# Memory outputs as high and low parts, and where the late gates end, in a hybrid decoder layer

## The chip, the cores and the metric

The kernel runs on one core of one Trainium2 chip. The metric is the device time of one execution in microseconds (us). A matrix product runs on TensorE (PE), with its weight loads beside it (PEld); VectorE is DVE, ScalarE ACT, GpSimd POOL, and SyncE (SP) issues most of the DMAs. Each of these engines works off its own queue of instructions in order.

## The reference

One decoder layer for 1024 tokens of width 1024. From one input projection come a sparse attention (8 heads of 64), a convolution branch and a cross-attention into 256 memory tokens (4 heads of 128). Each branch is projected to the width, weighted by a sigmoid gate, and the three are added; then follow the output projection and a SwiGLU feed-forward part.

```python
xn = rms_norm(x, norm_mix)
proj = xn @ w_in            # q, k, v, gates, conv inputs, memory queries, 3 merge gates
br_nsa = nsa_attention(q, kc, vc, ks, vs, kw, vw, gate) @ w_nsa_out
br_conv = silu(layer_norm(conv(glu(conv_in)))) @ w_conv_out
p_m = softmax(einsum('bshd,bmhd->bhsm', qm, km) * MEM_HEAD_DIM ** -0.5)
br_mem = einsum('bhsm,bmhd->bshd', p_m, vm).reshape(b, s, MEM_WIDTH) @ w_mem_out
gm = sigmoid(g_merge).reshape(b, s, N_BRANCH, D_MODEL)
h = x + (gm[:, :, 0] * br_nsa + gm[:, :, 1] * br_conv + gm[:, :, 2] * br_mem) @ w_out
return h + (silu(hn @ w_gate) * (hn @ w_up)) @ w_down      # hn = rms_norm(h, norm_ffn)
```

## The kernel before

**Arithmetic.** All is float32. A large product is made of three products of parts: an operand is split into a high part (a cast on ACT, L131) and a low part (the difference, L132, on DVE or POOL); `mm3` multiplies high by high, high by low and low by high (L146). An operand that was stored to DRAM whole has to be split again when it is loaded.

**Buffers.** `slab` is a pool of 16 buffers of 1 MB (128 partitions x 2048 words), used for the parts of activations; `wslab` (3) and `fslab` (2) hold split weights; `stage` (2 buffers named st) takes whole inputs of `unit` before they are split; `t4` and `t2` are small working tiles. PSUM banks come from `bank` (seven of them in turn), from `fbank` (one, the tile pf) or from `anybank` (all eight). A transfer into a buffer waits until the last reader of the former content is done.

**Order.** A scheduler orders the instructions of each engine by priorities and a model of their times; `follow(a, b)` and `add_manual_dep` add an order between two instructions. So an edit at one place can move others.

**Stages.** Input projections and key/value work; the memory attention in eight units of 256 tokens and two heads; the sparse attention in 16 groups (`for n in range(2 * NT)`: 128 tokens and one of two key groups each); the merge of the three branches (`branches`: memory, sparse attention, convolution); output projection; feed-forward part.

- A unit of the memory attention loads its queries from DRAM (L588) and splits them (`mem_qT`), makes scores, maxima and exponentials (`mem_softmax`, L609), turns the weights over through DRAM (`mem_squares`, `mem_load`), and multiplies by the values (`mem_out`). A copy on DVE (L645) takes the output from PSUM, and it is stored whole to `md`.
- The 24 merge gates (three branches of 8 column blocks, each `xn` by 128 columns of `w_in` in two halves of 24 products) are filler: they have a low priority. The first 12 (`N_EARLY`) may come anywhere, the late 12 are held to products of the attention (`anchors`): the j-th product of the late gates comes behind the anchor at which the share of the attention's work times 100/SPREAD is reached, with SPREAD = 97. A gate's half is copied from PSUM on ACT (L979, tile fz) and stored to `zd`.
- In attention, weights are transposed on PE against an identity (L918 for blocks, L904 for the compressed branch), taken from PSUM as parts (L131, L132), and multiplied by values. Some weights go through DRAM instead: `square_store` (L844) and `square_load` (L856, tensor `wd`). A group's output goes to `od` (L892).
- The memory merge loads the outputs `md` whole into st (L271), splits them into four slabs, and multiplies by `w_mem_out` (four units of 256 columns); each column block also loads its gate from `zd` (L1048) and takes its sigmoid (L1049). The casts of the last two outputs are held behind the last of `cmps`, the casts of the compressed branch's weights. The inputs of the next merge (from `od`) take the same path through st. The convolution's layer norm loads its inputs `ud` (L987).

## Time and profile before

| what | value |
|---|---|
| runs, us | 1701.01, 1700.6, 1700.25 (median 1700.6) |
| the profiled execution, us | 1696.93, of which the span is 1695.2 |
| mean granted clock of PE | 0.991 |
| PE busy | 97% of the span |
| chain that ended last | PE 53%, DVE 3%, DMA 2%, POOL 2%, ACT 1% |
| data moved | 262.11 MB, mean 155 GB/s |

In a row of the profile, `ps<-slab,fsl 128*128 128x512 x28` is output, operands, tile and shape, and the number of instructions; what stands in brackets is the idle time of the engine just before, and what ended it. In rows by stage come for each engine the busy time and (x) the number of instructions, then the clock granted to PE as a share of the full one, and the share and rate of the DMA. A group's mean time of a product can be above its step in a row of many, since products overlap: the step is the time of the row divided by its count.

### The profile page before, as it was taken

What the parts mean: (1) busy time and instruction counts of PE and PEld (TensorE: products, weight loads), DVE (VectorE), ACT (ScalarE), POOL (GpSimd) and SP (SyncE); (2) the same over time, 40 slices, a digit from 0 to 9 for tenths busy, and PEclk for the clock granted to TensorE, in tenths of its full rate; (3) what the DMA queues carried; (4) which work ended last, traced back from release to release, by engine and by line L of the source; (5) the groups of instructions that cost most, each with busy time, mean ns of one, the idle gap of its engine ahead of it and who ended that gap; (6) DMA issues with size and microseconds to landing.
All of it is one profiled execution on the core that took longest, in us unless ns stands there. A gap on an engine that the chain in (4) does not pass through costs nothing.

```text
span 1695.2 us, 22465 instructions
## 1 busy us (share of the span) xinstructions
PE 1650.6 (97%) x7904; PEld 1373.2 (81%) x7904; DVE 1064.8 (63%) x1800; ACT 729.8 (43%) x1343; POOL 642.6 (38%) x551
## 2 busy tenths in 40 slices
PE   7999999899999999998989999999999999999999
PEld 6887898787888888876867888888888888888887
DVE  6279888679556666865368626765545454466665
ACT  6311444342467767765356424532222323233332
POOL 0010012352267768764015401366556776400000
PEclk9999999999999999998989999999999999999999
DMA  8134345564255655545464313333233545793763
GB/s 282 40 96 132 124 143 174 160 194 136 77 160 147 166 171 166 165 133 178 170 215 150 107 50 132 96 114 118 91 109 118 168 143 178 268 402 125 228 234 123
DMA packets 247254, 262.11 MB, mean 155 GB/s; under 512 B 23956, under 2 KB 171716, under 8 KB 246118
## 3 DMA queue, kind: packets, MB, share of 16 engines
q1 hardware_dynamic: 240230, 248.10, 46.3%
q10 hardware_dynamic: 6912, 12.59, 2.0%
q8 instruction: 62, 1.02, 0.2%
q14 instruction: 50, 0.41, 0.1%
HBM read 181.99 MB, written 78.64 MB: 154 GB/s over the span
## 4 chain that ended last, share of the span: by engine, by line
PE 53%; DVE 3%; DMA 2%; POOL 2%; ACT 1%; issue 1%; SPq 0%; ACTq 0%; DVEq 0%; POOLq 0%
PE ps L146 34%; PE ps L1382 11%; PE pf L146 6%; PE pf L1382 1%; PE ps L918 1%; DMA st<-in_w_nsa_out_dram 1%; POOL slab L132 0%; DVE slab L132 0%; PE ps L236 0%; DMA t<-zd 0%; DMA st<-in_w_mem_out_dram 0%; DMA wd<-wsl 0%; POOL slab L729 0%; DVE t L1062 0%; POOL slab L1063 0%
## 5 line engine op out<-in xcount | busy, mean ns | idle before, releaser
L146 PE MATMUL ps<-slab,wsl 128*128 128x512 f32 (+1 forms) x1628 | 361.7, 381 | 0.0
L146 PEld LDWEIGHTS ps<-slab,wsl 128*128 128x128 f32 x1628 | 295.7, 188 | 59.7 <-issue 1.0
L146 PE MATMUL pf<-slab,fsl 128*128 128x512 f32 x1152 | 293.1, 395 | 2.0 <-ACT fz L979 1.8
L146 PEld LDWEIGHTS pf<-slab,fsl 128*128 128x128 f32 x1152 | 211.0, 188 | 43.9 <-ACT fz L979 3.4
L146 PE MATMUL ps<-slab,fsl 128*128 128x512 f32 x768 | 184.7, 395 | 10.5 <-ACT fsl L131 7.7
L146 PEld LDWEIGHTS ps<-slab,fsl 128*128 128x128 f32 x768 | 145.5, 190 | 43.5 <-ACT fsl L131 8.4
L447 DVE SCALAR_TENSOR_TENSOR slab<-slab,cw 128x1019 f32<-128x1019 f32 (+16 forms) x120 | 163.5, 1367 | 1.8
L146 PE MATMUL ps<-slab,slab 128*128 128x512 f32 (+1 forms) x616 | 150.7, 380 | 6.2 <-ACT slab L131 3.5
L1278 DVE TENSOR_TENSOR t<-ps,t 128x512 f32<-128x512 f32 x127 | 86.9, 688 | 108.1 <-PE ps L146 106.8
L146 PE MATMUL ps<-wsl,slab 128*128 128x512 f32 (+1 forms) x690 | 149.1, 365 | 0.5 <-DVE slab L228 0.3
L146 PEld LDWEIGHTS ps<-slab,slab 128*128 128x128 f32 x616 | 111.2, 190 | 29.4 <-ACT slab L131 4.0
L146 PEld LDWEIGHTS ps<-wsl,slab 128*128 128x128 f32 x690 | 117.4, 190 | 20.7 <-DVE t L645 0.6
L1382 PE MATMUL ps<-wsl 128*128 128x512 f32 x495 | 118.6, 389 | 0.0
L1382 PEld LDWEIGHTS ps<-wsl 128*128 128x128 f32 x495 | 92.9, 188 | 19.3
L132 DVE TENSOR_TENSOR wsl<-st,wsl 128x1024 fp32r<-128x1024 f32 x57 | 77.6, 1361 | 44.3 <-ACT wsl L131 43.4
L131 ACT CAST wsl<-st 128x1024 fp32r<-128x1024 f32 x58 | 60.9, 1051 | 89.4 <-PE ps L146 36.2
L146 PE MATMUL ps<-slab,qt 128*128 128x384 f32 (+6 forms) x400 | 93.8, 338 | 2.8 <-DVE sm L799 2.5
L146 PE MATMUL ps<-t,slab 128*128 128x256 f32 (+1 forms) x404 | 92.8, 332 | 2.4 <-DVE t L132 1.6
L1063 POOL TENSOR_TENSOR slab<-slab,t 128x512 f32<-128x512 f32 x32 | 48.1, 1521 | 113.4 <-DVE t L1062 113.4
L131 ACT CAST wsl<-t 128x1024 fp32r<-128x1024 f32 x43 | 45.3, 1054 | 90.6 <-POOL t L128 36.4
L1291 POOL TENSOR_TENSOR t<-t,t 128x512 f32<-128x512 f32 x21 | 40.0, 1906 | 112.4 <-DVE t L1278 44.9
L132 DVE TENSOR_TENSOR t<-ps,t 128x512 fp32r<-128x512 f32 (+2 forms) x96 | 60.9, 639 | 30.6 <-ACT t L131 29.7
(252 smaller groups left out, 2810.5 us busy)
## 6 DMA issues: line engine op xcount, KB each, us to landing
t<-in_w_down_dram SPq DMA_DIRECT2D x70, 256.0 KB, 4.1
fst<-in_w_in_dram SPq DMA_DIRECT2D x24, 512.0 KB, 4.5
zd<-fz ACTq DMA_DIRECT2D x48, 256.0 KB, 3.4
slab<-wd SPq DMA_DIRECT2D x24, 512.0 KB, 4.4
t<-zd SPq DMA_DIRECT2D x24, 512.0 KB, 3.4
st<-in_w_gate_dram SPq DMA_DIRECT2D x22, 512.0 KB, 3.9
st<-in_w_up_dram SPq DMA_DIRECT2D x22, 512.0 KB, 4.2
ad<-t SPq DMA_DIRECT2D x44, 256.0 KB, 2.8
```

The lines of the kernel that those rows point to most:

```text
L131: m = nc.scalar.copy(hi, src)
L132: return m, (eng or nc.vector).tensor_tensor(lo, src, hi.bitcast(F32), op=OP.subtract)
L146: m = nc.tensor.matmul(o, a, b, start=start, stop=stop)
L447: return nc.vector.scalar_tensor_tensor(acc[:, s:], u[:, :S - s], cw[:, ct, 30 - s:31 - s], acc[:, s:], op0=OP.mult, op1=OP.add)
L918: nc.tensor.transpose(b[:, j - j0, h, :], tiles[h][:, j * P:(j + 1) * P], ident)
L1063: nc.gpsimd.tensor_tensor(a, a, z, op=OP.add)
L1278: nc.vector.tensor_tensor(o, a_, b_, op=OP.add)
L1291: nc.gpsimd.tensor_tensor(u4, u4, c22, op=OP.mult)
L1382: nc.tensor.matmul(B[t], a_, b_, start=start and k == 0 and j == 0, stop=k == FH - 1 and j == 2, skip_group_check=True)
```

## The change

Memory outputs are now split where they are made: `mem_out` casts the output from PSUM into the slab that held the weights, makes the low part on DVE, and stores both to `md`, which is twice as large (16 stores of 256 KB for 8). They are loaded as parts, 1 MB each, straight into four slabs (`mem_in`, L955) in the last step of attention that makes scores, behind the last square load written by then; the casts and low parts of the memory merge's inputs and `cmps` are gone. SPREAD is 84 instead of 97, and all gates use `fbank`. Queries of the memory attention are loaded two units ahead (`mem_qload`), and their casts come behind the exponentials of the unit before. The `ud` loads follow the last square load, the sigmoids the last exponential, and the second halves of the memory merge's first four blocks may use any bank. The number of products is the same.

```diff
--- before
+++ after
@@ -33,3 +33,3 @@
 N_EARLY = 12
-WB, SPREAD = 6, 97
+WB, SPREAD = 6, 84
 TAP_LEAD = 12
@@ -198,3 +198,3 @@
     od = drp.tile([4, P, S], F32, tag="od", name="od")
-    md = drp.tile([4, P, S], F32, tag="md", name="md")
+    md = drp.tile([4, P, 2, S], F32, tag="md", name="md")
     qraw = drp.tile([2, NT, P, 512], F32, tag="qraw", name="qraw")
@@ -265,3 +265,3 @@
 
-    def unit(src, shape, alloc=wslab, eng=None, load=False, after=None):
+    def unit(src, shape, alloc=wslab, eng=None, load=False):
         if alloc is fslab:
@@ -272,5 +272,3 @@
         w = alloc([2] + shape)
-        m, _ = split(w[:, 0], w[:, 1], st, eng)
-        if after is not None:
-            follow(m, after, "cast behind")
+        split(w[:, 0], w[:, 1], st, eng)
         return (w, ld.ins) if load else w
@@ -584,9 +582,15 @@
 
-    def mem_qT(hp, tp):
-        QM, raw = t4([2, 2, 2, 4, 32], F32R), t2([2, 4, 2, 32])
+    def mem_qload(u):
+        raw = t2([2, 4, 2, 32])
         for tt in range(2):
-            nc.sync.dma_start(raw[:, tt],
-                              qt_m[2 * tp + tt, :, :, :, 64 * hp:64 * hp + 64].rearrange("c r a (h s) -> (c r) a h s", h=2))
+            nc.sync.dma_start(raw[:, tt], qt_m[2 * (u % 4) + tt, :, :, :, 64 * (u // 4):64 * (u // 4) + 64].rearrange(
+                "c r a (h s) -> (c r) a h s", h=2))
+        return raw
+
+    def mem_queries(raw):
+        QM = t4([2, 2, 2, 4, 32], F32R)
         for tt in range(2):
-            split(QM[:, 0, tt], QM[:, 1, tt], raw[:, tt].rearrange("p a h s -> p h a s"), nc.gpsimd)
+            m, _ = split(QM[:, 0, tt], QM[:, 1, tt], raw[:, tt].rearrange("p a h s -> p h a s"), nc.gpsimd)
+            if exps:
+                follow(m, exps[-1], "queries behind the exponentials")
         return QM
@@ -643,5 +647,7 @@
                     VM[:, 1, mb, hh * P:(hh + 1) * P], ph, pl, mb == 0, mb == 1)
-        om = t2([2, 256])
-        nc.vector.tensor_copy(om, o)
-        nc.sync.dma_start(md[2 * hp:2 * hp + 2, :, tp * 256:(tp + 1) * 256].rearrange("h p t -> p h t"), om)
+        om = [PT[:, hl, 0].rearrange("p a h t s -> p (a h t s)").rearrange("p (h t) -> p h t", h=2) for hl in range(2)]
+        split(om[0], om[1], o)
+        for hl in range(2):
+            nc.sync.dma_start(md[2 * hp:2 * hp + 2, :, hl, tp * 256:(tp + 1) * 256].rearrange("h p t -> p h t"),
+                              om[hl].bitcast(F32))
 
@@ -649,7 +655,11 @@
 
-        QM, PT = {0: mem_qT(0, 0)}, {}
+        raws, PT = [mem_qload(0), mem_qload(1)], {}
+        QM = mem_queries(raws.pop(0))
         for u in range(8):
+            if u < 6:
+                raws.append(mem_qload(u + 2))
+            pm = mem_softmax(u // 4, u % 4, QM)
             if u < 7:
-                QM[u + 1] = mem_qT((u + 1) // 4, (u + 1) % 4)
-            mem_squares(u // 4, u % 4, mem_softmax(u // 4, u % 4, QM[u]))
+                QM = mem_queries(raws.pop(0))
+            mem_squares(u // 4, u % 4, pm)
             queries(ws, u, 1, rqn)
@@ -731,2 +741,3 @@
     QS, OB, QN, PC, WT, WP, WF, anchors, behind, tails = {}, {}, {}, {}, {}, {}, {}, [], [], []
+    squares = []
     wd = drp.tile([2 * NT, 20, 32, 4, P], F32, tag="wd", name="wd")
@@ -855,4 +866,5 @@
         n = o.shape[1]
-        nc.sync.dma_start(o.bitcast(F32).rearrange("p j a h q -> p j (a h q)"),
-                          wd[2 * i + g, 4 * j0:4 * (j0 + n)].rearrange("(j b) k a q -> (b k) j (a q)", b=4))
+        squares.append(nc.sync.dma_start(
+            o.bitcast(F32).rearrange("p j a h q -> p j (a h q)"),
+            wd[2 * i + g, 4 * j0:4 * (j0 + n)].rearrange("(j b) k a q -> (b k) j (a q)", b=4)).ins)
 
@@ -905,3 +917,3 @@
             pt = t2([4, P], F32R)
-            cmps.append(split(pt[:64], pt[64:], b[:64])[0].ins)
+            split(pt[:64], pt[64:], b[:64])
             m = mm(o.rearrange("p h q -> p (h q)"), vcmp[:, g, :], pt.rearrange("p h q -> p (h q)"), True, False)
@@ -926,3 +938,2 @@
 
-    cmps = []
     load_q(0, 0)
@@ -940,2 +951,6 @@
                 turn_q((n + 1) // 2, (n + 1) % 2)
+            if step == 4 * (2 * NT - 1) + 3:
+                mem_in = [slab([2, S]) for k in range(4)]
+                for k in range(4):
+                    follow(nc.sync.dma_start(mem_in[k].bitcast(F32), md[k]), squares[-1], "behind the squares")
             tiles = scores(i, g, br, hp)
@@ -971,3 +986,3 @@
             for h_ in range(2):
-                ps = (bank if n_ > 20 and h_ else fbank)([512])
+                ps = fbank([512])
                 for k in range(KT):
@@ -986,3 +1001,3 @@
         for ct in range(4):
-            nc.sync.dma_start(U[ct][:, 1], ud[ct])
+            follow(nc.sync.dma_start(U[ct][:, 1], ud[ct]), squares[-1], "behind the last squares")
 
@@ -1032,3 +1047,3 @@
     branches = ((2, w_mem_out), (0, w_nsa_out), (1, w_conv_out))
-    nxt, conv = [unit(md[k], [S], alloc=slab, after=cmps[-1] if k > 1 else None) for k in range(4)], []
+    nxt, conv = mem_in, []
     steps = layer_norm(conv)
@@ -1048,6 +1063,6 @@
                 nc.sync.dma_start(zz, zd[br, d_])
-                nc.scalar.activation(zz, zz, AF.Sigmoid)
+                follow(nc.scalar.activation(zz, zz, AF.Sigmoid), exps[-1], "behind the last exponential")
                 for half in range(2):
                     z = zz[:, half * 512:(half + 1) * 512]
-                    ps = (anybank if n_ else bank)([512])
+                    ps = (anybank if n_ or dp < 2 and half else bank)([512])
                     for k in range(4):
```

**ACT in the memory attention**, at the fourth unit. L609 (L613 after) is an exponential, L341 and L345 (L339, L343) belong to another projection, and `t4<-t2 128x256` on L131 is the cast of half a unit's queries. Before:

```order
L341 COPY t2_312_2203<-ps_311_2178 128x512
L345 ACTIVATE t2_313_2204<-ps_311_2178 128x512
L131 CAST t4_301_2132<-t2_302_2133 128x256
L609 ACTIVATE t4_303_2140,sm_306_2143<-ps_308_2145,sm_305_2142 128x256 x2
L609 ACTIVATE t4_303_2140,sm_306_2143<-ps_309_2153,sm_305_2142 128x256 x2
```

After:

```order
L131 CAST slab_285_2036<-ps_299_2117 128x512
L613 ACT_TABLE_LOAD
L613 ACTIVATE t4_302_2139,sm_305_2142<-ps_307_2144,sm_304_2141 128x256 x2
L613 ACTIVATE t4_302_2139,sm_305_2142<-ps_308_2152,sm_304_2141 128x256 x2
L131 CAST t4_309_2170<-t2_286_2038 128x256 x2
```

The query cast stood ahead of the exponentials and stands behind them now; before them comes the cast of a memory output from PSUM (`slab_285<-ps_299`), which is new.

**PE where the last group's blocks are transposed** (L918 before, L930 after). Rows with t4 and a slab are products by values. Before:

```order
L918 MATMUL ps_1261_6442<-identr_107,slab_1225_6266 128x128 x4
L904 MATMUL ps_1259_6433<-identr_107,t2_1224_6265 64x128 x2
L146 MATMUL ps_1213_6207<-t4_1255_6410,slab_393_2677 128x512
L918 MATMUL ps_1263_6454<-identr_107,slab_1225_6266 128x128 x4
L918 MATMUL ps_1265_6466<-identr_107,slab_1225_6266 128x128 x4
L146 MATMUL ps_1213_6207<-slab_1212_6204,slab_393_2677 128x512
L146 MATMUL ps_1213_6207<-t4_1255_6410,slab_393_2677 128x512
L146 MATMUL ps_1213_6207<-slab_1212_6204,slab_393_2677 128x512
L146 MATMUL ps_1213_6207<-t4_1235_6305,slab_393_2677 128x512 x2
L918 MATMUL ps_1267_6478<-identr_107,slab_1225_6266 128x128 x4
L146 MATMUL ps_1258_6432<-t2_1260_6438,vcmp_136 128x512
```

After, where the slabs 1237 to 1240 are memory outputs, fsl_1438 a unit of memory weights:

```order
L930 MATMUL ps_1257_6458<-identr_107,slab_1217_6274 128x128 x4
L916 MATMUL ps_1255_6449<-identr_107,t2_1216_6273 64x128 x2
L146 MATMUL ps_1205_6215<-t4_1251_6426,slab_386_2684 128x512
L930 MATMUL ps_1259_6470<-identr_107,slab_1217_6274 128x128 x4
L930 MATMUL ps_1261_6482<-identr_107,slab_1217_6274 128x128 x4
L146 MATMUL ps_1440_8132<-slab_1237_6366,fsl_1438_8125 128x512 x2
L146 MATMUL ps_1441_8146<-slab_1237_6366,fsl_1438_8125 128x512 x2
L146 MATMUL ps_1443_8163<-slab_1237_6366,fsl_1438_8125 128x512 x2
L146 MATMUL ps_1205_6215<-slab_1204_6212,slab_386_2684 128x512
L146 MATMUL ps_1205_6215<-t4_1251_6426,slab_386_2684 128x512
```

The first transpositions were followed by products of the group before alone; now six products of the memory merge stand behind the third. The last gate products were further on in the queue:

```order
L146 MATMUL pf_1421_7970<-slab_23_196,fsl_1420_7967 128x512
L146 MATMUL pf_1421_7970<-slab_24_197,fsl_1420_7967 128x512 x6
L146 MATMUL pf_1421_7970<-slab_25_198,fsl_1420_7967 128x512 x6
L146 MATMUL pf_1421_7970<-slab_26_199,fsl_1420_7967 128x512 x6
L146 MATMUL ps_1423_7998<-slab_64_405,fsl_1420_7967 128x512
L146 MATMUL ps_1423_7998<-slab_65_406,fsl_1420_7967 128x512 x6
L146 MATMUL ps_1477_8296<-slab_1430_8032,fsl_1475_8290 128x512 x2
L146 MATMUL ps_1478_8310<-slab_1430_8032,fsl_1475_8290 128x512 x2
L146 MATMUL ps_1481_8331<-slab_1430_8032,fsl_1475_8290 128x512 x2
L146 MATMUL ps_1482_8345<-slab_1430_8032,fsl_1475_8290 128x512 x2
L146 MATMUL ps_1477_8296<-slab_1430_8032,fsl_1475_8290 128x512
```

These are rows in the memory merge before: pf_1421 and ps_1423 are gates (by fsl_1420), ps_1469 to ps_1482 the merge; fsl_1475 is the fourth unit of memory weights. After, this is the place:

```order
L146 MATMUL ps_1461_8270<-slab_1238_6367,wsl_1446_8193 128x512 x3
L146 MATMUL ps_1461_8270<-slab_1239_6368,wsl_1446_8193 128x512 x3
L146 MATMUL ps_1461_8270<-slab_1240_6369,wsl_1446_8193 128x512 x3
L146 MATMUL ps_1465_8292<-slab_1237_6366,fsl_1463_8286 128x512 x2
L146 MATMUL ps_1466_8306<-slab_1237_6366,fsl_1463_8286 128x512 x2
L146 MATMUL ps_1469_8327<-slab_1237_6366,fsl_1463_8286 128x512 x2
L146 MATMUL ps_1470_8341<-slab_1237_6366,fsl_1463_8286 128x512 x2
```

No gate stands there. The last gate products are now these, ahead of the last group's values:

```order
L146 MATMUL pf_1419_8014<-slab_62_403,fsl_1416_7983 128x512 x6
L146 MATMUL pf_1419_8014<-slab_63_404,fsl_1416_7983 128x512 x6
L146 MATMUL pf_1419_8014<-slab_64_405,fsl_1416_7983 128x512
L146 MATMUL ps_1142_5945<-t4_1165_6042,slab_386_2684 128x512
L146 MATMUL pf_1419_8014<-slab_64_405,fsl_1416_7983 128x512 x5
L930 MATMUL ps_1212_6249<-identr_107,slab_1155_6003 128x128 x4
L146 MATMUL pf_1419_8014<-slab_65_406,fsl_1416_7983 128x512 x6
L146 MATMUL ps_1224_6296<-slab_383_2680,qt_1153_5999 128x448 x2
```

So the gates end some 120 rows earlier against the fourth unit of weights, here fsl_1463.

**SP around the loads of the memory outputs.** L271 loads into st, L844 (L855) and L856 (L867) are square stores and loads, L892 (L904) stores a group's output. Before:

```order
L271 DMA st_1431_8035<-md_141 128x1024
L844 DMA wd_3285<-wsl_1211_6200 32x16x128 x4
L844 DMA wd_3285<-wsl_1194_6137 32x4x128 x4
L856 DMA slab_1257_6429<-wd_3285 128x2x512 x2
L271 DMA st_1433_8040<-md_141 128x1024
L271 DMA st_1435_8045<-md_141 128x1024
L892 DMA od_140<-t2_1256_6425 64x4x128
L271 DMA st_1437_8050<-in_w_mem_out_dram 128x4x256
L856 DMA t4_1269_6490<-wd_3285 128x512
L271 DMA st_1449_8127<-in_w_mem_out_dram 128x4x256
L271 DMA st_1457_8195<-in_w_mem_out_dram 128x4x256
```

After:

```order
L904 DMA od_140<-t2_1194_6180 64x4x128
L867 DMA t4_1227_6313<-wd_3293 128x512
L955 DMA slab_1237_6366<-md_141 128x2048
L955 DMA slab_1238_6367<-md_141 128x2048
L955 DMA slab_1239_6368<-md_141 128x2048
L955 DMA slab_1240_6369<-md_141 128x2048
L271 DMA st_1437_8123<-in_w_mem_out_dram 128x4x256
L271 DMA st_1445_8191<-in_w_mem_out_dram 128x4x256
L855 DMA wd_3293<-wsl_1203_6208 32x16x128 x4
L855 DMA wd_3293<-wsl_1186_6145 32x4x128 x4
L867 DMA slab_1253_6445<-wd_3293 128x2x512 x2
L904 DMA od_140<-t2_1252_6441 64x4x128
```

The four loads of `md` were spread over the last two groups, 512 KB each; now they stand in a row, 1 MB each, ahead of the last two square stores and the last large square load, with two loads of weights (st) behind them.

## The prediction

> **What bounds the kernel now.** I read the page first, then the busy time by stage, then what TensorE (PE) waits for, then the timeline at each wait.
>
> ```profile
> span 1695.2 us, 22465 instructions
> PE 1650.6 (97%) x7904; PEld 1373.2 (81%) x7904; DVE 1064.8 (63%) x1800; ACT 729.8 (43%) x1343; POOL 642.6 (38%) x551
> core 0: us, PE busy (x) PEld busy (x) DVE busy (x) ACT busy (x) POOL busy (x), PEclk, DMA share, GB/s
> 300.00:450.00 150.00, 142.76 (x692) 118.01 (x691) 110.45 (x174) 53.23 (x129) 51.72 (x44) 0.99 0.47 143
> 450.00:750.00 300.00, 294.15 (x1622) 250.33 (x1621) 198.55 (x711) 214.35 (x540) 218.41 (x236) 1.00 0.55 158
> 750.00:800.00 50.00, 41.86 (x206) 33.40 (x206) 31.34 (x69) 28.81 (x51) 24.34 (x19) 0.86 0.48 150
> 800.00:846.00 46.00, 46.00 (x205) 37.74 (x204) 13.13 (x17) 14.10 (x16) 2.77 (x2) 1.00 0.52 186
> 846.00:875.00 29.00, 21.44 (x82) 16.79 (x82) 17.77 (x21) 15.71 (x17) 0.00 (x0) 0.82 0.69 218
> 875.00:925.00 50.00, 47.19 (x202) 37.54 (x201) 42.99 (x37) 30.07 (x29) 23.11 (x14) 1.00 0.49 159
> 925.00:1695.00 770.00, 766.50 (x3413) 634.99 (x3412) 427.40 (x509) 258.74 (x340) 289.26 (x193) 1.00 0.47 156
> ```
>
> PE is busy 97% of the span, and the change takes no product away. So all that can be won is PE's idle time, 1695.2 − 1650.6 = 44.6 us, and the time in which its granted clock is below 1. The stages that the change touches hold 7.2 us idle (300 to 450), 5.9 (450 to 750), 8.1 (750 to 800, clock 0.86) and 7.6 (846 to 875, clock 0.82). After 925 only 3.5 us are idle, at clock 1.00; nothing is to be won there. Over 300 to 930 the longest waits of PE are these (total us, times, longest):
>
> ```profile
> PE ps L146 <- ACT fsl L131: 7.7, 2, 7.6
> PE ps L918 <- DVE t L132: 5.8, 5, 3.6
> PE ps L146 <- ACT slab L131: 4.1, 3, 2.3
> PE pf L146 <- ACT fz L979: 1.8, 3, 0.7
> ```
>
> The first lies in the memory merge, the second in attention's tail, the third in the memory attention. I take them as terms A, B and C in order of time.
>
> **A, the memory attention (300 to 450).**
>
> ```profile
> 302.74 0.41 ACT L131 CAST t<-t 128x256 fp32r<-128x256 f32 x1 [4.50 <-DMA t<-qt_m]
> 321.04 0.41 ACT L131 CAST t<-t 128x256 fp32r<-128x256 f32 x1 [4.55 <-DMA t<-qt_m]
> 305.96 0.39 PE L146 MATMUL ps<-slab,slab 128*128 128x256 f32 x1 [1.21 <-ACT slab L131]
> 307.80 0.65 PE L146 MATMUL ps<-slab,t 128*128 128x256 f32 x2 [1.45 <-ACT t L131]
> 325.68 0.39 PE L146 MATMUL ps<-slab,slab 128*128 128x256 f32 x1 [2.33 <-ACT slab L131]
> 308.00:311.00 3.00, 3.00 (x9) 2.41 (x9) 3.00 (x4) 0.23 (x1) 2.61 (x2) 0.50 0.23 87
> ```
>
> ACT stands 4.5 us at a query cast whose load has not landed, twice. The exponentials are queued behind that cast, and PE waits for the weights made from them. With loads two units ahead and the cast behind the exponentials, ACT has nothing to stand at: 1.21 + 1.45 + 2.33 = 5.0 us of waits go, and 3.00 us at clock 0.50 give back 1.5, so −6.5. Against it stand the parts of the outputs, made eight times:
>
> ```profile
> L645 DVE COPY t<-ps 128x512 f32<-128x512 f32 x8 | 5.4, 679 | 4.0 <-PE ps L146 4.0
> L132 DVE TENSOR_TENSOR t<-ps,t 128x512 fp32r<-128x512 f32 x64 | 43.3, 684 | 26.9 <-ACT t L131 26.6
> L131 ACT CAST slab<-ps 128x512 fp32r<-128x512 f32 x20 | 10.8, 595 | 6.4 <-PE ps L236 4.1 <-PE ps L577 1.9 <-POOL t L132 0.4
> ```
>
> DVE makes the low part (684 ns) instead of the copy (679 ns): nothing. ACT gains 8 × 0.595 = 4.8 us of casts in a stage of 150 us where it is busy 53; SP gains eight stores. Where a cast falls between a product and an exponential it can cost PE up to its 0.6 us, at three units of the eight 1.8; that is the cover's price. I take **−5**, between −6.6 and +1 (no wait gone, and two new ones of 0.6).
>
> **B, attention's tail (750 to 800).**
>
> ```profile
> 756.34 0.66 PE L918 MATMUL ps<-identr,slab 128*128 128x128 f32 x4 [0.81 <-DVE t L132]
> 757.61 0.73 PE L146 MATMUL ps<-slab,qt 128*128 128x512 f32 x2 [0.61 <-DVE sm L799]
> 759.00:760.00 1.00, 1.00 (x6) 1.00 (x6) 1.00 (x7) 0.69 (x2) 0.00 (x0) 0.50 0.00 0
> 774.72 0.66 PE L918 MATMUL ps<-identr,slab 128*128 128x128 f32 x4 [0.95 <-DVE t L132]
> 779.01 1.12 PE L918 MATMUL ps<-identr,slab 128*128 128x128 f32 x4 [3.63 <-DVE t L132]
> 774.92 3.43 DVE L132 TENSOR_TENSOR slab<-st,slab 128x1024 fp32r<-128x1024 f32 x2 [0.25 <-ACT slab L131]
> 773.84 1.99 ACT L131 CAST slab<-st 128x1024 fp32r<-128x1024 f32 x2
> 779.00:789.00 10.00, 8.51 (x29) 6.60 (x30) 5.01 (x6) 5.17 (x7) 1.68 (x2) 0.50 0.62 224
> ```
>
> The transposes of the last group wait 3.63 us for DVE's low part of the tile before them, and DVE is at two low parts of memory outputs for 3.43 us, ACT at their casts for 1.99. Behind that wait PE runs at 0.50 for 10 us: 8.51 × 0.5 = 4.3 us lost. An earlier dip, around 759, loses 1.7 (3.4 us at 0.50, by the windows of one microsecond). Idle 8.1 and clock 6.0 make 14.1 us in this stage.
>
> After, these casts and low parts are not there. What is late next is the tile's own chain, cast 0.6 and low part 0.7 behind a transposition, which already costs 0.81 and 0.95 where it stands alone; the 3.63 becomes about 1.2. I keep the other waits: 8.1 − 2.4 = 5.7 idle, and one dip of 1.7; that is a gain of 6.7. But the last group loses its gates: until the first merge product stand 10.3 us of small products and transpositions (counted in the order, 0.235 us for 512 columns from the row of 19 gate products below, shorter ones in proportion) with nothing long between them. I take 1 us off: **−6**, from −11 (only two waits of 1 us left) to 0 (waits as now).
>
> One rule stands against this term. The Trainium skill, TensorE: Matmul & The Clock Gate, Part 4 (PE-mode transpose), says that a transposition doesn't count as PE-busy for the clock gate as a product does. The trace neither shows nor excludes it: the dip at 759 comes behind transpositions and behind two waits alike. By the rule B would be the thin group below; by the rows it is the −6.
>
> **C, the memory merge (846 to 875).**
>
> ```profile
> 845.79 1.05 ACT L131 CAST slab<-st 128x1024 fp32r<-128x1024 f32 x1 [6.88 <-PE pf L146]
> 857.88 1.04 ACT L131 CAST fsl<-st 128x1024 fp32r<-128x1024 f32 x1 [2.44 <-DMA st<-in_w_mem_out_dram]
> 845.36 4.47 PE L146 MATMUL pf<-slab,fsl 128*128 128x512 f32 x19
> 858.98 9.14 PE L146 MATMUL ps<-slab,fsl 128*128 128x512 f32 x28 [7.56 <-ACT fsl L131]
> 854.00:864.00 10.00, 5.02 (x12) 3.95 (x13) 4.76 (x7) 5.25 (x5) 0.00 (x0) 0.51 0.87 297
> ```
>
> The fourth unit of memory weights comes late, since its stage buffer held attention outputs whose casts waited 6.88 us for slabs that the late gates still read. PE idles 7.56 us, and 28 products then take 9.14 us where 28 × 4.47/19 = 6.6 would do: 10.1 us in all. After, the gates end in the last group but one, and the slabs are free. What is late next is the last group's own output: behind its last product stand 73 products until the fourth unit's first, 73 × 0.235 = 17.2 us. In that time must pass: copy and difference (0.6 + 0.7), store (0.6 to issue, 3.0 to land), load, cast and low part of the output, then load and cast of the weights.
>
> ```profile
> od<-t SPq DMA_DIRECT2D x16, 128.0 KB, 3.0
> st<-od SPq DMA_DIRECT2D x1, 512.0 KB, 3.6
> st<-in_w_mem_out_dram SPq DMA_DIRECT2D x3, 512.0 KB, 3.8
> ```
>
> 0.6 + 0.7 + 3.6 + 3.6 + 1.05 + 1.7 + 3.8 + 1.04 = 16.1 us, issues of 0.4 each not counted. It fits by a hair; I allow a stall of 1 us (0 to 5): **−9**, from −10 to −5.
>
> **The rest.** More gates come into 450 to 750 (16.5 instead of 13), where DVE, ACT and POOL are busy 199, 214 and 218 of 300 us: room enough. With one bank the second half of a gate waits for the copy of the first; three such waits cost 1.8 us now, and I add as much again: +2 (0 to +4). From 875 to 925 PE idles 50 − 47.2 = 2.8 us, in the merge of the next branch, which the order leaves as it is; it stays.
>
> **The sum.** −5 − 6 − 9 + 2 = −18. On the profiled execution, 1696.93 us (1.7 outside the span), that is 1679; it ran 3.7 us below the median of 1700.6, so the median becomes **1683**.
>
> **Rivals.**
> *A thin last group.* Without gates the clock falls to half for all the 10.3 us before the first merge product: 10.3 more, of which 1.7 is counted, so +8.6: 1691. For: 0.81 + 0.61 us of waits were enough for a dip at 759. Against: it lasted 3.4 us, and products went on. (The rule of the Trainium skill named under B, TensorE: Matmul & The Clock Gate, Part 4, speaks for this rival.)
> *The change doesn't do what it says:* the fourth unit is late still, because the stage buffers pass through the attention outputs as before. C gives 1 instead of 9: 1691. For: the margin of 1 us. Against: the 6.88 us of waiting for slabs has no cause left. With both rivals 1699, no change.
> *Slower: the loads of the memory outputs.* They are now 4 × 1 MB, on SP behind the last squares but those of the last half group, in slabs that come free near the end of the gates, and ahead of the stores and loads of the last squares. The fourth is needed some 17 us later (10.3 us of products, 2 of waits, 19 products). At the best slice of the stretch from 740 to 800,
>
> ```profile
> GB/s 183 271 326 286 151 23 214 376 109 0 0 0 87 18 157 0 0 11 0 22 213 329 333 264 98 206 404 433 325 0 87 23 344 339 168 44 305 11 0 183
> ```
>
> 433 GB/s, 4.19 MB take 9.7 us; at the mean from 750 to 800, 150 GB/s, 28. Then PE stands 11 us, runs half for 10 (5 lost), and B gains nothing: −5 − 9 + 16 + 2 = +4: 1705. It decides from some 27 us for the four loads, 155 GB/s. For: the rate of now. Against: that is what was asked for, not what the queue can do.
>
> **Chances.** Forecast 0.60 (1674 to 1688), thin group 0.15, fourth unit late 0.10, both 0.07, slower 0.08. A measurement of this kernel tells some 0.2% (3.4 us) from no change: faster 0.85, same 0.07, slower 0.08. The range 1674 to 1695 takes in the first three; its low end is all terms but one near their best.
>
> **What would show it.** A: no ACT wait of 4 us for qt_m at 302 and 321. B: at the last group's transpositions waits near 1 us, no wait of 3.6, no low parts slab<-st between them; a wait of the first merge products on a DMA of md speaks for the slower case. C: no wait over 5 us for a weight cast in the memory merge, clock near 1.00 there. I am wrong if the gates, now denser, let PE idle over 10 us from 450 to 750, or if a new wait of over 8 us appears in the tail.

## The result and the profile after

The changed kernel took 1673.4 us in the median of four runs (1671.7 to 1675.5) against 1700.4 (the three runs of before with a fourth), a ratio of 0.984 (95% interval 0.983 to 0.986): 27 us faster. The forecast was 1683, and the range from 1674 missed the median by 0.6 us. On another chip the same two kernels stood at 1673.5 and 1698.2, 24.7 us apart (ratio 0.985, 0.984 to 0.987).

The page after, and the busy time by stage in the same stretches as before:

```profile
span 1672.0 us, 22478 instructions
PE 1638.8 (98%) x7904; PEld 1368.8 (82%) x7904; DVE 1067.7 (64%) x1796; ACT 730.2 (44%) x1347; POOL 642.0 (38%) x551
...
300.00:450.00 150.00, 142.04 (x706) 117.24 (x705) 119.78 (x225) 61.35 (x166) 59.43 (x62) 1.00 0.51 155
450.00:750.00 300.00, 298.14 (x1631) 257.36 (x1630) 187.83 (x637) 203.08 (x493) 204.60 (x214) 1.00 0.51 154
750.00:800.00 50.00, 44.95 (x245) 37.57 (x244) 30.79 (x80) 27.57 (x53) 24.52 (x22) 0.97 0.72 237
800.00:846.00 46.00, 43.14 (x203) 34.80 (x202) 26.85 (x32) 24.25 (x26) 6.14 (x3) 1.00 0.73 255
846.00:875.00 29.00, 29.00 (x125) 23.29 (x125) 23.80 (x24) 18.15 (x18) 9.90 (x6) 1.00 0.51 163
```

PE's idle time fell from 44.6 to 1672.0 − 1638.8 = 33.2 us, and its busy time by 11.8 us for the same products. The memory attention (first row) idles 8.0 us where it idled 7.2. The stretch from 450 to 750 idles 1.9 us, not 5.9, and the later rows hold one dip of the clock of 3.4 us (0.97; another comes at 901), where one of 3.4 and two of 10.2 us stood (0.86 and 0.82).

The waits of PE from 270 to 930, after (total us, times, longest):

```profile
PE ps L146 <- DVE t L132: 3.2, 6, 1.3
PE ps L930 <- DVE t L132: 2.4, 2, 1.5
PE ps L146 <- DVE slab L132: 2.4, 1, 2.4
PE ps L146 <- POOL slab L132: 2.2, 2, 1.4
PE ps L146 <- ACT t L131: 1.9, 3, 1.3
...
PE ps L146 <- DVE slab L1075: 1.5, 1, 1.5
PE ps L146 <- ACT fsl L131: 1.0, 1, 1.0
```

The wait of 7.6 us for weights (fsl) is 1.0, and that of 3.6 at the transpositions (L930) is at most 1.5. The wait for POOL's low parts of the memory attention's weights grew from 0.7 to 2.2 us, and 1.5 us for a bank (L1075, the product with the gate on DVE) are new. In the timeline of PE the places that the prediction named look like this:

```profile
785.96 0.66 PE L930 MATMUL ps<-identr,slab 128*128 128x128 f32 x4 [0.95 <-DVE t L132]
788.08 1.11 PE L930 MATMUL ps<-identr,slab 128*128 128x128 f32 x4 [1.46 <-DVE t L132]
...
818.71 3.04 PE L146 MATMUL ps<-slab,fsl 128*128 128x512 f32 x12 [1.50 <-DVE slab L1075]
...
837.27 6.69 PE L146 MATMUL ps<-slab,fsl 128*128 128x512 f32 x28 [1.02 <-ACT fsl L131]
```

The last row is the fourth unit of memory weights: a wait of 1.02 us (1 was forecast), and its 28 products take 6.69 us (6.6) instead of 9.14. ACT's timeline has the cast of the last attention output and the unit's own:

```profile
831.90 1.05 ACT L131 CAST slab<-st 128x1024 fp32r<-128x1024 f32 x1 [1.27 <-DMA st<-od]
...
836.17 1.05 ACT L131 CAST fsl<-st 128x1024 fp32r<-128x1024 f32 x1 [0.24 <-DMA st<-in_w_mem_out_dram]
```

To compare runs whose stages lie at different times, I add up PE's **loss** in windows of one microsecond: idle time, and busy time multiplied by what the clock lacks to 1. The stages are cut at the work itself: the memory attention from 15 us before its first exponential up to the first product with a query tile of the sparse attention; the groups up to 35 us before the last such product; the tail up to the last product by values; the merge up to 1000 us. The last column is the span without the loss, which is PE's busy time brought to full clock. What lies before it is the first 240 us; 3.6 to 4.1 us at the end of each run are left out.

| run | median us | first 240 | memory att. | groups | tail | merge | at full clock |
|---|---|---|---|---|---|---|---|
| before | 1700.6 | 10.7 | 9.2 | 5.3 | 14.7 | 13.1 | 1638.5 |
| before again (e1) | 1698.7 | 11.3 | 9.9 | 5.4 | 12.3 | 16.3 | 1638.6 |
| early gates alone (e2) | 1689.3 | 11.3 | 12.5 | 5.5 | 14.3 | 7.1 | 1635.9 |
| early gates and parts (e3) | 1675.4 | 11.0 | 13.2 | 3.2 | 3.2 | 6.4 | 1633.1 |
| early queries alone (e4) | 1677.2 | 8.6 | 5.2 | 5.4 | 12.7 | 5.5 | 1635.0 |
| gates before third pair (e5) | 1690.7 | 9.7 | 11.1 | 4.9 | 13.9 | 6.8 | 1638.0 |
| after | 1673.4 | 8.3 | 8.8 | 2.0 | 7.1 | 6.7 | 1635.4 |
| after again (e9) | 1673.5 | 9.3 | 10.0 | 1.8 | 7.6 | 5.8 | 1636.4 |
| after, no follows (e6) | 1670.9 | 10.9 | 9.9 | 1.8 | 3.7 | 8.7 | 1633.5 |
| the same again (e10) | 1671.2 | 8.7 | 9.2 | 1.8 | 3.1 | 7.2 | 1634.5 |
| after, old queries (e7) | 1675.3 | 8.5 | 11.4 | 3.1 | 7.4 | 4.0 | 1633.8 |
| after, whole outputs (e8) | 1674.3 | 9.4 | 4.9 | 2.3 | 15.1 | 5.3 | 1630.6 |
| no follows, gates to 88 (e11) | 1670.0 | 10.9 | 8.2 | 1.8 | 2.5 | 4.0 | 1633.4 |
| the same again (e14) | 1670.5 | 11.6 | 12.3 | 1.8 | 2.4 | 5.9 | 1631.7 |
| no follows, gates to 78 (e12) | 1681.0 | 11.2 | 8.2 | 1.8 | 13.5 | 7.4 | 1634.0 |
| as e14, casts behind (e13) | 1668.3 | 10.9 | 8.6 | 1.8 | 2.7 | 7.3 | 1631.2 |

### The profile page after: what moved, and what is told of

Its sections match the earlier page's. It is cut to its first block, busy times and chain, and to the rows that moved or that the text cites. A ratio compares the mean times of both kernels' runs of the same rounds, so it can differ in the third digit from the quotient of the medians.

```text
span 1672.0 us, 22478 instructions
## 1 busy us (share of the span) xinstructions
PE 1638.8 (98%) x7904; PEld 1368.8 (82%) x7904; DVE 1067.7 (64%) x1796; ACT 730.2 (44%) x1347; POOL 642.0 (38%) x551
## 3 DMA queue, kind: packets, MB, share of 16 engines
q8 instruction: 62, 1.02, 0.2%
## 4 chain that ended last, share of the span: by engine, by line
PE 85%; DVE 6%; DMA 3%; ACT 3%; issue 2%; POOL 1%; SPq 0%; DVEq 0%; POOLq 0%; ACTq 0%
PE ps L146 52%; PE pf L146 17%; PE ps L1397 11%; PE ps L930 2%; DVE slab L445 2%; PE pf L1397 1%; PE ps L236 1%; DMA t<-zd 1%; DVE fsl L132 0%; POOL t L619 0%; ACT t L131 0%; DMA qraw<-t 0%; DVE t L132 0%; DMA st<-in_w_nsa_out_dram 0%; DMA wd<-wsl 0%
## 5 line engine op out<-in xcount | busy, mean ns | idle before, releaser
L146 PE MATMUL pf<-slab,fsl 128*128 128x512 f32 x1248 | 315.0, 394 | 1.7 <-ACT fz L994 1.7
L146 PEld LDWEIGHTS pf<-slab,fsl 128*128 128x128 f32 x1248 | 228.9, 188 | 46.3 <-ACT fz L994 2.8
L445 DVE SCALAR_TENSOR_TENSOR slab<-slab,cw 128x1019 f32<-128x1019 f32 (+16 forms) x120 | 168.6, 1408 | 1.5
L146 PE MATMUL ps<-slab,fsl 128*128 128x512 f32 x672 | 162.1, 397 | 5.0 <-DVE slab L132 2.4
L146 PEld LDWEIGHTS ps<-slab,fsl 128*128 128x128 f32 x672 | 127.5, 191 | 34.0 <-DVE slab L132 3.3
L131 ACT CAST wsl<-st 128x1024 fp32r<-128x1024 f32 x58 | 60.9, 1051 | 78.6 <-PE ps L146 33.1
L146 PE MATMUL ps<-t,slab 128*128 128x256 f32 (+1 forms) x404 | 89.4, 320 | 3.2 <-DVE t L132 3.1
L131 ACT CAST wsl<-t 128x1024 fp32r<-128x1024 f32 x43 | 45.3, 1053 | 86.1 <-POOL t L128 33.1
```

The source lines that it names most:

```text
L131: m = nc.scalar.copy(hi, src)
L146: m = nc.tensor.matmul(o, a, b, start=start, stop=stop)
L445: return nc.vector.scalar_tensor_tensor(acc[:, s:], u[:, :S - s], cw[:, ct, 30 - s:31 - s], acc[:, s:], op0=OP.mult, op1=OP.add)
```

## The experiments

**e1, the kernel before again.** No edit. 

> The kernel before, unchanged, profiled a second time. PE's loss (idle time plus busy time at a clock below 1) was 56.7 us in the first profile, 10.1 of it in the first 30 us, of which 1.7 at half clock. If the profiled execution of before was a fast one by chance (it ran 3.7 us below the median of its runs), this profile runs at 1699 to 1701 and its loss in the stages is the same within 1 us, so that the rest must lie in PE's busy time at full clock. If the profile's 1697 is typical of profiled executions, it comes again within 1 us. Ratio 1.000 within 0.002.

Measured: ratio 1.000 (0.999 to 1.001), the profiled execution at 1699.2 us. So the first profile, at 1696.9, came out some 2 us low by chance; total loss 58.9 against 56.7, single stages apart by up to 3.2 us (between e11 and e14, also one kernel, by 4.1). Differences below that in one stage of one profile decide nothing.

**e2, early gates alone**, and **e3, with outputs as parts**, both from before:

```diff
-WB, SPREAD = 6, 97
+WB, SPREAD = 6, 84
-                ps = (bank if n_ > 20 and h_ else fbank)([512])
+                ps = fbank([512])
```

e3 adds the edits of `md`, `mem_out`, `squares` and `mem_in`, and nothing else of the change.

> Before with SPREAD 84 and all gates in the one bank; nothing else. Theory: the early end of the gates alone frees the slabs, so the 7.6 us wait for the fourth unit of memory weights goes (C: loss 10.3 to 2, -8), and the denser gates fill the attention's groups (5.8 us idle to 2.5, -3.5); the tail keeps its 3.6 us wait behind the low parts of memory outputs (loss 14 stays or grows by 1 to 3 for want of gates). Sum -9 to -12: about 1690. Rival (the tail's gain is from the gates too, or the parts are needed for C): -15 or more, or under -5.

> As the run with early gates alone, and memory outputs as parts, loaded straight into slabs; queries, sigmoids and the loads of the convolution as before. Theory: the parts take casts and low parts out of the tail, so against early gates alone another -6 to -8 (tail loss 14 to 7), and the memory attention gains nothing or loses 1: about 1682. Rival (parts give nothing of their own, what moved is the schedule): within 3 us of the run with early gates alone.

Measured: 1689.3 (ratio 0.995, 0.993 to 0.996) and 1675.4 (0.986, 0.984 to 0.988). e2 came out as its theory said in time and in the merge, whose loss falls to 7.1; the groups stay at 5.5, of which 3.8 are idle time (5.3 and 5.4 in the two profiles of before) and 1.7 one dip of the clock. e3 gained 14 us over e2 where 6 to 8 were expected: the parts take 11 us out of the tail. The wait behind the casts of memory outputs is in the timeline of e2, as in that of before, and in that of e8 below, where only the outputs are whole:

```profile
798.73 1.12 PE L918 MATMUL ps<-identr,slab 128*128 128x128 f32 x4 [3.66 <-DVE t L132]
```

```profile
781.71 1.12 PE L930 MATMUL ps<-identr,slab 128*128 128x128 f32 x4 [3.65 <-DVE t L132]
```

In the timeline of DVE of e8 the two low parts stand ahead of the tile's:

```profile
777.59 3.46 DVE L132 TENSOR_TENSOR slab<-st,slab 128x1024 fp32r<-128x1024 f32 x2 [0.25 <-ACT slab L131]
780.98 0.68 DVE L132 TENSOR_TENSOR t<-ps,t 128x512 fp32r<-128x512 f32 x1
```

No run with parts has a wait above 1.5 us at a transposition of attention's blocks.

**e4, early queries alone** (from before: `mem_qload`, `mem_queries` and the new loop in `mem_attention`). 

> Before with only the queries of the memory attention loaded two units ahead and cast behind the exponentials. The prediction's term A said -5. The profile of after shows PE's loss in the memory attention as it was (8.8 us before, 8.8 after), so: theory 'the early loads are worth it, and the parts eat the gain': -5 to -6.5 here. Rival 'the wait only passes on to the next link (POOL's parts of the weights, 0.8 and 1.4 us in the profile of after)': within 2 us of no change.

Measured: 1677.2 (0.987, 0.985 to 0.989), far beyond both. The memory attention's loss falls to 5.2, so the early loads are worth their 4 to 5 us here. Most of the rest is in the merge, whose loss falls to 5.5, although the gates may end as late as before; 3.5 us are busy time at full clock. ACT's timeline in e4 shows why:

```profile
815.59 1.06 ACT L131 CAST slab<-st 128x1024 fp32r<-128x1024 f32 x1 [6.41 <-PE pf L146]
...
829.26 1.05 ACT L131 CAST fsl<-st 128x1024 fp32r<-128x1024 f32 x1 [4.61 <-DMA st<-in_w_mem_out_dram]
```

The cast of the first attention output waits 6.41 us for a gate here too (6.88 before). But the scheduler put the last gate of that bank ahead of the third pair of the merge's column blocks, not behind it. Before, that cast came 33.6 us behind the last product by values (845.79 against 812.22), here 19.7 (795.9). PE has work until the fourth unit is there.

**e5, the same swap by itself.** From before:

```diff
+                last_gate = products[-1][0]
...
+                        if n_ == 0 and dp == 2 and k == 0:
+                            tc.add_manual_dep(first.ins, last_gate.name, ORDER, reason="behind the last gate")
```

> Before, with the third pair of column blocks of the memory merge (48 products) held behind the last gate product; on PE this swaps these 48 products with the 26 gate products that stood behind them, and nothing else ahead of them. Theory: the stall of C (7.6 us, and 2.5 us of half clock) came of these gate products alone, which held the slabs that the attention outputs' parts waited for, and so the stage buffer that the fourth unit of memory weights waited for; 48 products are 10.9 us, so the unit comes 10.9 us earlier against its use: loss behind the last attention product from 13 to about 4, -8 to -10 us, 1690. Rival (the fourth unit waits for the last group's output on its way through DRAM, gates or not): -2 or less.

Measured: 1690.7 (0.994, 0.993 to 0.996), 9.6 us less, as its theory said; the merge's loss is 6.8, the tail's and the groups' are as before. ACT's timeline:

```profile
834.22 1.05 ACT L131 CAST slab<-st 128x1024 fp32r<-128x1024 f32 x1 [0.61 <-PE pf L146]
...
846.88 1.05 ACT L131 CAST fsl<-st 128x1024 fp32r<-128x1024 f32 x1 [0.93 <-DMA st<-in_w_mem_out_dram]
```

The cast comes at 834.22, not 845.79, and the unit's own at 846.88, not 857.88. Gates that were laid aside for 48 products were nearly the whole of term C. Early gates, early queries and this swap each remove it, which is why their gains don't add up.

**e6, after without the two orders and the third bank rule:**

```diff
-            follow(nc.sync.dma_start(U[ct][:, 1], ud[ct]), squares[-1], "behind the last squares")
+            nc.sync.dma_start(U[ct][:, 1], ud[ct])
-                follow(nc.scalar.activation(zz, zz, AF.Sigmoid), exps[-1], "behind the last exponential")
+                nc.scalar.activation(zz, zz, AF.Sigmoid)
-                    ps = (anybank if n_ or dp < 2 and half else bank)([512])
+                    ps = (anybank if n_ else bank)([512])
```

> After, without the order of the convolution loads and of the sigmoids, and with the memory merge's banks as before. Theory: these edits have no share: within 2 us of after, 1672 to 1676, PE's loss in the stages as in after (memory attention 8.8, groups 2.0, tail 7.1, merge 6.7). Rival: they keep SP and ACT free for the tail, and the tail loses 3 or more: 1677 or over.

**e7, after with the old queries**, and **e8, after with whole outputs** (each part of the diff undone):

> After with the queries of the memory attention as before (one unit ahead, casts where they stood). Theory: the early queries are worth 4.5 us also beside the parts: memory attention's loss from 8.8 to about 13, 1678. Rival (the profile's reading that their gain is eaten by the parts): within 2 us of after, 1672 to 1676.

> After with memory outputs stored whole and split in the tail, as before. Theory: the casts and low parts come back into the tail: its loss from 7.1 to 13 or 14, the memory attention's from 8.8 to about 8 at most: 1679 to 1681. Rival (the tail's gain is from the gates' place): within 2 us of after.

Measured: e6 1670.9 (0.983, 0.982 to 0.984), below both expectations, its tail's loss 3.7, so these edits don't help, and rather harm the tail; in time the intervals of e6 and after overlap. e7 1675.3 (0.985, 0.984 to 0.987) and e8 1674.3 (0.985, 0.984 to 0.986) came in where their rivals said: each part on top of the others is worth 1 or 2 us, which the intervals don't tell from none. By stages they do work: without parts the tail is back at 15.1, as the theory of e8 said, but the memory attention falls from 8.8 to 4.9 and the busy time at full clock by 5. With the old queries the memory attention is at 11.4.

The loss in the memory attention, averaged over the profiles of the table (without e13), shows how the two edits depend on each other: 10.7 with old queries and whole outputs (4 profiles), 12.3 with old queries and parts (2), 5.1 with early queries and whole outputs (2), 9.5 with both (7). So the early queries gain 5.6 beside whole outputs and 2.8 beside parts, and the parts cost 1.6 beside old queries and 4.4 beside early ones.

**e9 to e12**, one chip: after again; e6 again; and e6 with SPREAD 88 and 78.

> After, unchanged, on the chip of the next three runs. 1671 to 1676; a second profile shows by how much the stages' losses scatter (memory attention 8.8, groups 2.0, tail 7.1, merge 6.7 in the first): within 1.7 us each, one clock dip.

> The run without the two orders and without the third bank rule, again. If its 2.5 us below after is real, as its tail says (waits of 0.95 and 1.46 at the last group's transpositions are not there, 3.7 for 7.1), then 1670 to 1672 and 2 to 3 below after on this chip; if it was the chip, within 1 of after.

> The same with SPREAD 88. Theory (the more gate products lie in the attention groups the less PE idles there, and gates in the last groups cover its waits): groups' loss as at 84, 1.8 to 3, tail 2 to 4; the loads of the memory outputs come later, since their slabs come free later: 1670 to 1674. Rival, the prediction's slower case: the loads of 4 MB are late and PE waits for them, a wait of 3 us or more on a DMA of md, 1676 or over.

> The same with SPREAD 78. The last two groups have no gates then: theory (they need them as filler): tail's loss up from 3.7 to 6 or more, groups 1 to 2, 1673 to 1676. Rival (a thin group costs nothing): 1671 or less. By the prediction's thin-group rival (half clock through a group without gates) 1680 or over.

Measured: 1673.5, 1671.2, 1670.0 and 1681.0 (ratio of the last 0.991, 0.989 to 0.992). e10 repeats e6's 2 to 3 us below after, and its tail (3.1, where after has 7.1 and 7.6); the intervals of e9 and e10 overlap. At 88 no PE wait on a load of `md` appears: the slower rival isn't seen. Outputs as parts with gates ending at 97 were not tried, since the loads then need slabs that late gates hold. At 78 the time is above what the theory said, in the range of the thin-group rival, and the tail's loss is 13.5. These are its waits from 748 to 824:

```profile
PE ps L146 <- DVE t L132: 4.7, 4, 1.9
PE ps L146 <- DVE sm L810: 3.2, 3, 1.6
PE ps L146 <- DVE fsl L132: 1.9, 1, 1.9
```

With the gates gone some 9 us earlier (the last at 758, in e10 at 768), PE waits for maxima (sm) and low parts at places that gates covered: 10.1 us idle and 3.4 of clock, two single dips. So the rival's time came, but not by its mechanism, half clock through the group. The filler pays where it lies beside short dependent work.

**e13, the cast of a memory output behind the exponentials**, and **e14, the same kernel without that move** (SPREAD 88 again). The edit of e13:

```diff
+        def parts():
+            m, _ = split(om[0], om[1], o)
+            if late:
+                follow(m, exps[-1], "output parts behind the next exponentials")
...
             pm = mem_softmax(u // 4, u % 4, QM)
+            if late_parts:
+                late_parts.pop()()
```

> As the run whose gates end at 88, with the cast of a memory output held behind the next unit's exponentials on ACT (it stood just ahead of them and waited 1.5 to 2.8 us for PE there). Theory: the parts eat the queries' gain because this cast, waiting for PE, stands ahead of the exponentials that the next scores, transposes and products hang on: the memory attention's loss falls from 8.2 to 4 or 6, the rest as it was, -2 to -4. Rival (the loss there comes from the order on POOL and PE, the exponentials wait for DVE's maxima anyway): 7 to 9 as before, time within 1.5 us.

> The run whose gates end at 88, again, beside it on the same chip: 1668 to 1672; loss in the memory attention 8 to 10, groups 1.8, tail 2 to 4, merge 4 to 6.

Measured: 1668.3 (0.982, 0.981 to 0.984) and 1670.5 (0.983, 0.982 to 0.984). ACT's timeline in e14:

```profile
341.94 0.59 ACT L131 CAST slab<-ps 128x512 fp32r<-128x512 f32 x1 [1.46 <-PE ps L146]
345.39 0.48 ACT L613 ACTIVATE t<-ps,sm 128x256 f32<-128x256 f32 x1 [2.87 <-DVE sm L609]
```

In e13, ACT's exponentials of the same unit, and then PE:

```profile
337.57 0.48 ACT L613 ACTIVATE t<-ps,sm 128x256 f32<-128x256 f32 x1
```

```profile
348.46 5.97 PE L146 MATMUL ps<-wsl,slab 128*128 128x512 f32 x18 [4.00 <-DVE slab L132]
```

The exponentials come 7.8 us earlier, and these waits of PE in e14 are gone or smaller (0.70, none and 0.24 us in e13; e11, the same kernel as e14, has the first two and not the third):

```profile
315.36 0.80 PE L146 MATMUL ps<-slab,t 128*128 128x256 f32 x4 [1.30 <-ACT t L131]
...
340.25 1.59 PE L146 MATMUL ps<-slab,slab 128*128 128x256 f32 x11 [1.34 <-POOL slab L132]
...
388.21 0.54 PE L696 MATMUL ps<-identr,t 128*128 128x128 f32 x4 [2.40 <-DVE t L132]
```

In their place PE (the last row of e13 above) stands once for 4.00 us, for a bank that DVE's low part of the output still has to read; on DVE it came at 347.75, behind 3.35 us of the convolution's work (L445). The loss of 8.6 is not the 4 to 6 of the theory but what the rival said. Against e14's 12.3 it looks like a gain, but 3.4 of the 12.3 are clock, and e11 has 8.2; idle time alone is 7.0 in e13, 8.9 in e14 and 8.2 in e11. The time is 2.2 us below e14, and the intervals overlap. So moving the cast moves PE's waits; that it gains time is not shown, and how much of the 4 to 5 us hangs on the cast's place stays open.

## Why the prediction was wrong

By means of the two profiles of each kernel, with the forecast's terms:

| term | forecast | measured |
|---|---|---|
| A, memory attention | −5 | 9.4 − 9.6 = −0.2 |
| groups, gates denser | +2 | 1.9 − 5.4 = −3.5 |
| B, tail | −6 | 7.4 − 13.5 = −6.1 |
| C, merge (and the next one's 2.8, 0) | −9 | 6.3 − 14.7 = −8.4 |
| first 240 us | 0 | 8.8 − 11.0 = −2.2 |
| busy time at full clock | 0 | 1635.9 − 1638.6 = −2.7 |
| sum | −18 | −23.1 |

The medians differ by 27.0 us, and by 24.7 on the other chip: the profiled executions of before ran 3.7 us below and 0.5 above the medians beside them, those of after 0.4 and 2.8 above, so up to 4 us lie in no term. That the range was missed by 0.6 us is within that scatter; what was wrong is in the terms.

**B and C were right** in mechanism and size. The tail's wait of 3.63 us was DVE's, for the low parts of memory outputs: it is in every run with whole outputs (3.62 to 3.66) and in none with parts. It became 1.46 (1.2 forecast), and in the runs with parts but without the two orders and the bank rule it is not there at all. C was the chain from late gates over slabs and the stage buffer to the fourth unit; e5 shows it alone. Only the reason for it was told too narrowly: not the share 97 itself, but that two half gates were laid aside behind 48 products, which the schedule of e4 undoes by the way.

**The step that failed is "The rest": "+2 (0 to +4)".** I counted what one bank could cost the groups and left out what more gate products could gain. The waits of PE in the groups before (448 to 750) and after (433 to 770):

```profile
PE ps L146 <- DVE sm L799: 1.9, 4, 0.9
PE ps L146 <- DVE t L132: 1.4, 4, 0.6
PE pf L146 <- ACT fz L979: 1.2, 2, 0.7
```

```profile
PE ps L146 <- DVE sm L810: 0.8, 3, 0.3
...
PE pf L146 <- ACT fz L994: 0.6, 2, 0.5
PE ps L146 <- DVE t L132: 0.2, 1, 0.2
```

The waits for the bank (fz) fell from 1.2 to 0.6 us, where 2 more were forecast, and the waits for maxima and low parts shrank from 3.3 to 1.0. By the order on PE, 26 gate halves lie between the first and the last score before, 28 in e4 and 30 in e2, where the groups lose 4.9 to 5.5; in the runs with 32 to 34 halves they lose 1.8 to 3.2. Idle time alone is 4.9 to 5.4 with 26 halves, some 3.8 with 28 and 30, and 1.8 to 3.2 from 32 on. That goes with the number of gates, but no run changed it alone, since each change also moved the order, so it is not shown to be the cause: that stays open.

**A was mis-sized by its cover.** "−5, between −6.6 and +1" is the 6.5 of the waits less some 1.5 for the parts, whose price was put at up to 1.8. The early queries alone are worth 4 to 5 (e4), or more (e8 against e2: 12.5 to 4.9); but beside them the parts take 4 to 5 back (e8 against after), more than twice their price. The wait that A named is gone (PE's 2.33 us at 325.68, and ACT's waits for qt_m fell from 12.4 to 1.1 us from 240 to 440); others took its place, for POOL's low parts and at casts on ACT.

**Two terms were missing.** "All that can be won is PE's idle time and the time below full clock" is false by 2.7 us: the busy time at full clock is 1638.0 to 1638.6 in the three profiles whose attention is ordered as before, and 1630.6 to 1636.4 in all others. Counted from the start of one PE instruction to that of the next, the 473 transpositions of 128 columns take 2.1 us less (47.1 to 45.0) and the 112 products of 384 columns 1.6 less (22.3 to 20.7), while products of 512 columns stay within 1 us; what shortens them is not settled. And 1.7 us of the first stretch are one dip of the clock, which is there or not in executions of the same kernel (1.4 in e6, 0 in e10), so most of that term's 2.2 us is luck.

**The rivals.** The thin last group did not come, although the stretch without gates took 19.0 us with its waits (769.85 to 788.84), where 10.3 of products were counted: from 775 to 786, within it, PE is busy 8.14 of 11 us at full clock. One dip follows, as counted; in the second profile (e9) the whole tail has none. Below that row are windows of 3.41 us around the two waits of 0.95 and 1.46 us, first in after, then in e9:

```profile
775.00:786.00 11.00, 8.14 (x51) 6.43 (x51) 7.87 (x25) 8.46 (x17) 9.35 (x9) 1.00 1.00 393
...
784.68:788.09 3.41, 1.01 (x7) 0.46 (x6) 1.38 (x2) 1.88 (x3) 3.41 (x4) 1.00 1.01 283
788.09:791.50 3.41, 3.41 (x10) 2.88 (x11) 2.70 (x1) 0.15 (x1) 1.80 (x1) 0.50 0.99 291
```

```profile
787.17:790.58 3.41, 1.91 (x13) 1.26 (x11) 0.69 (x1) 1.66 (x3) 3.41 (x4) 1.00 0.96 275
790.58:793.99 3.41, 2.50 (x13) 1.93 (x14) 2.99 (x2) 1.08 (x2) 2.77 (x2) 1.00 1.14 344
```

In after both waits fall into one window, PE is busy 1.01 us of it, and the next window runs at half clock. In e9 the border of two windows lies between the waits, and the clock stays full.

The Trainium skill's rule on this (TensorE: Matmul & The Clock Gate, Part 4: a transposition doesn't count as PE-busy in the same way) would, taken strictly, have the clock fall there. The rows do not bear it out for transpositions mixed with short products: of the 1.91 us in e9's first window 1.47 are transpositions (by the tile identr), and without them PE would be busy 13% of it; half clock followed every window of so little work (see the last section). A stretch of transpositions alone was not run.

The row from 775 to 786 also answers the slower rival: the DMAs moved 393 GB/s then, not 150, and no product of the merge waited for a load of `md`. The fourth unit was late by 1.02 us, as the margin said, but partly by luck: from the last product by values (to 817.2) to the end of the weight cast (837.2) the chain took 20.0 us, not 16.1, and PE's own wait of 1.50 us for a bank hid some of that. In e9 it took 21.4 us, and the unit was 2.52 us late.

The range held each term to its own bounds, but the groups' bound was on the wrong side of zero. With the measured −3.5 in place of its 0, the low end would have been near 1670.

## What to carry to other kernels

Filler products can cover short dependent work, so where they end is worth trying in both directions: at 84 and 88 the slabs that they hold come free in time for the merge, and at 78 the tail lost 10 us again. (That the groups lose less because they hold more gates is not shown.) A wait at the end of a chain of buffers can be removed in several ways, so gains of edits measured alone must not be added: alone, early gates gave 10 us and early queries 22, together with the rest 27. Moving a split out of a crowded tail is a gain only as far as the place it moves to has room on the engine that it waits on, here ACT and a PSUM bank. Of the versions run, after without the two orders and the bank rule, with gates to 88 and the output casts behind the exponentials, had the lowest median: 1668.3, against 1673.4; the same without the move of the casts had 1670.0 and 1670.5, which the intervals don't tell from it.

## What the hardware showed

Stretches at half clock come and go between executions of one program: e11 and e14, the same kernel, differ by 3.4 us of clock loss in the memory attention. In the clock records of all 16 profiles (up to 1000 us) a dip is 3.41, 6.83, 10.24 or 13.65 us long at 0.50, that is one to four windows, and costs up to 1.7 us for each; within an execution all dips start on one grid of 3.41 us, which lies differently in each execution. The Trainium skill (TensorE: Matmul & The Clock Gate, Part 1) tells of a free-running window of 3.4 us, which agrees.

On these grids, from 240 to 1000 us, 3474 windows ran at full clock. Half clock followed all 29 in which PE was busy less than 45% of the window, 14 of the 43 from 45 to 60%, and none of the others. So some 1.4 to 1.9 us of waits within one window can bring a dip (before had one at 758.55, behind a window with PE busy 1.99 of 3.41 us), and the same waits bring none where a border divides them, as in e9 above. A term of a forecast should take a single dip as a chance of 1.7 us, not as a certainty.
